# A one-core hybrid SSD and attention block: how q and k leave PSUM, where the first bias columns lie, and when eight modulation columns are computed

## The chip, the cores and the metric

The kernel runs on one core of a Trainium2 chip. A core has a matrix engine (TensorE, PE in the profile; its weight loads are shown as PEld), a vector engine (VectorE, DVE), an activation engine (ScalarE, ACT), a general engine (GpSimd, POOL) and a sync engine (SyncE, SP), which issues most of the DMAs here. Each engine takes its instructions strictly in the order in which the program lists them, and they wait for each other by semaphores. The metric is the device time of one execution in microseconds (us), taken as the median of several runs.

## The reference, cut to what matters

One layer with a state-space (SSD) group, an attention group and a feed-forward part. The change touches the attention group and the modulation vector `mod`, which is a product of a row vector with a matrix of 1024 x 6144.

```python
c_act = jax.nn.silu(c)
mod = (c_act @ w_ada[l] + b_ada[l])[:, None, :]
sh_m, sc_m, g_m, sh_f, sc_f, g_f = jnp.split(mod, 6, axis=-1)
h = rmsnorm(x, norm_mix_w[l]) * (1 + sc_m) + sh_m
z, xbc, dt_raw, q, k, v = jnp.split(h @ w_in[l], IN_SPLITS, axis=-1)
...
# chunk_attention: 8 heads of 64, chunks of 64 rows, own chunk + 8 before
scores = einsum('bcqhd,bckhd->bhcqk', qc, kb) * (ATTN_HEAD_DIM ** -0.5)
bias = rel_bias[:, rel_idx]          # clipped relative position
p = softmax(where(valid, scores + bias, min))
o = einsum('bhcqk,bckhd->bcqhd', p, vb)
```

The sequence has 1024 rows, the model 1024 columns, and everything is float32.

## The kernel before, in words

A product of two float32 matrices is made of three products of rounded parts (`mm3`, L79 to L82): each operand is split into a high part, rounded by an ACT copy, and a low part, which DVE computes as the operand minus the high part (`split`, L84 to L90).

The stages run in this order. **Stage 0** (about 0 to 97 us): x is loaded, normalized and transposed; the first 16 modulation columns are computed, one row of `w_ada` at a time, by `mod_col` (L136), which loads 512 KB by an SP DMA and reduces it on DVE against a row buffer `rowa`; and the q, k and v of head pairs 0 and 1 are computed from `w_first` in two halves of 512 rows (the `for hh in range(2)` loop), with four PSUM accumulators `accs`, n = 0 to 3, for q and k of pair 0 and of pair 1. **Attention** (about 97 to 280 us): `attention(p)` for the four head pairs; in each, four steps u of two blocks of 128 query rows (i = 2u and 2u + 1). `attn_scores` computes the scores of a block on PE (`scores`, L258), adds the bias and takes the row minimum of the negated sum on DVE (L494), takes the exponential on ACT (L497), the reciprocal on DVE (L499) and normalizes on POOL (L500). `attn_pv` transposes the result on PE (L526, L529), splits it (L89, L90) and multiplies it with v (L537, L538). While pair 1 and pair 2 run, `gemm_part` computes q, k and v of the next pair (`acc`, one PSUM bank; the second half of 512 rows can start only when the first has been taken out of it). **Convolution** (`conv_silu`, about 267 to 370 us) follows with 24 to 25 modulation columns between, and then the SSD part, the output projection and the feed-forward part, which the change doesn't touch.

Around the change:

- `evac_qkv` (L220) takes q, k or v of one pair and one half out of PSUM. The score product wants, for each of the two heads, a q tile whose one half of the partitions holds the high part and the other half the low part, and tiles `kh` and `kl` that hold the same 64 rows on both halves of the partitions. The accumulator has head 0 on partitions 0 to 63 and head 1 on 64 to 127. For q the kernel before uses two ACT instructions (L226) and two DVE instructions (L228) on 64 partitions each, and no DMA. For k it uses two ACT (L232), two DVE (L235), and four SP DMAs (L233, L236) that copy 64 x 512 numbers to the other half of the partitions. This is done 16 times: for q and k, four pairs, two halves.
- `attention` loads two bias tiles of 128 x 640 for its pair (L555), masks two corners on POOL (L556, L557), and the DVE of L494 reads them. The pools of attention are opened when those of stage 0 are closed, on the same memory.
- `rowb` is the second half of the tile `rows_`. It is used at the start (`diag`, until about 8 us) and again after the convolution (L846).
- In pair 3, `attention` calls `mod_col` `MODS` = (0, 1, 1, 5) times in its steps, into four free q/k buffers; each is placed behind the last reciprocal of the step's scores. After each convolution column tile, `conv_mods` calls it `CMODS` times.
- The order of the instructions on each engine is set when the program is built: a planner walks through the program with estimated durations and, on each engine, issues what is ready by its estimate, earlier program text first. GEMMs of a next stage are thus pulled forward to fill PE. [...]

Of the kernel before, what the change touches and what calls it, by code (L numbers as in the profile page):

```python
# [25 lines left out]
WZB = 4  # L26
PB = (2, 2, 0, 4)
GRID = 1.5 * 2.0 ** 17
MODS = (0, 1, 1, 5)
CMODS = (2, 3, 3, 3, 3, 3, 4, 4)  # L30
PRST = 4
GP, GPL = {0: (0,1), 2: (2,)}, ()
XL = (3, 4, 5, 6)
# [11 lines left out]
def f32(ap):  # L45
    return ap.bitcast(F32)
# [22 lines left out]
def tile_block(ctx: ExitStack, tc: tile.TileContext, x, ccol, pk, w_ada, w_first, w_ft, w_z,  # L69
               w_out, w_up, w_down, bias, fnw, out, dbg=None):  # L70
    nc = tc.nc
    V, A, T = (InOrder(tc, e) for e in (nc.vector, nc.scalar, nc.tensor))
    G = nc.gpsimd
# [28 lines left out]
    rowa, rowb = rows_[:, 0, :], rows_[:, 1, :]  # L102
# [33 lines left out]
    def mod_col(ft, t, at=None):  # L136
        nc.sync.dma_start(t, w_ada[ft])
        with tc.issue_after(at) if at else ExitStack():
            V.tensor_tensor_reduce(out=t, in0=t, in1=rowa, scale=1.0, scalar=0.0,
                                   op0=ALU.mult, op1=ALU.add, accum_out=modc[:, ft:ft + 1])  # L140
# [35 lines left out]
    es_at = ExitStack()  # L176
# [5 lines left out]
    s0 = es_0.enter_context(tc.tile_pool(name="s0", bufs=1, side="right"))  # L182
# [33 lines left out]
    def new_pair(p):  # L216
        qk[p] = {n: [qk_tile(F32R) for _ in range(2)] for n in ("q", "kh", "kl")}
        qk[p]["v"] = vv[:, :, p % 2]

    def evac_qkv(p, which, hh, ps, tmp, tps):  # L220
        d = qk[p]
        c = slice(hh * 512, hh * 512 + 512)
        rows = ((slice(0, 64), slice(64, 128)), (slice(64, 128), slice(0, 64)))
        if which == 0:
            for q, (r, o) in zip(d["q"], rows):
                A.activation(q[r, c], ps[r, :], AF.Copy, scale=0.125)  # L226
            for q, (r, o) in zip(d["q"], rows):
                V.scalar_tensor_tensor(q[o, c], ps[r, :], 0.125, f32(q[r, c]), op0=ALU.mult,  # L228
                                       op1=ALU.subtract)
        elif which == 1:  # L230
            for kh, (r, o) in zip(d["kh"], rows):
                A.activation(kh[r, c], ps[r, :], AF.Copy)  # L232
                nc.sync.dma_start(f32(kh[o, c]), f32(kh[r, c]))  # L233
            for kh, kl, (r, o) in zip(d["kh"], d["kl"], rows):
                V.tensor_tensor(kl[r, c], ps[r, :], f32(kh[r, c]), ALU.subtract)  # L235
                nc.sync.dma_start(f32(kl[o, c]), f32(kl[r, c]))  # L236
# [101 lines left out]
    for j in range(2):  # L338
# [9 lines left out]
                           op0=ALU.add, op1=ALU.mult)  # L348
# [34 lines left out]
    for hh in range(2):  # L383
        accs = [(ps0, ps0b)[n // 2].tile([P, 512], F32, tag="acc0", bufs=2, name="acc0") for n in range(4)]
        vps = [psv.tile([P, 2, 256], F32, tag=t, bufs=1, name="vps") for t in ("acc", "pv")]
        split_at = KT - (2, 4)[hh]
        tail = range(split_at, KT)
        for kt in range(KT):
            if hh == 0:
# [77 lines left out]
    pp = es_at.enter_context(tc.tile_pool(name="pp", bufs=8, side="right", reuse_waits="tile"))  # L467
    bp = es_at.enter_context(tc.tile_pool(name="bp", bufs=3, side="right", reuse_waits="tile"))
    ptp = es_at.enter_context(tc.tile_pool(name="ptp", bufs=1, side="right", reuse_waits="tile"))
    pst = es_p1.enter_context(tc.tile_pool(name="pst", bufs=1, space=PSUM, side="right",  # L470
                                           reuse_waits="tile"))
    ya = yp.tile([P, NT, 512], F32, tag="y", name="ya")
# [6 lines left out]
    def tp_tile():  # L479
        return pst.tile([P, 512], F32, tag="tp", bufs=2, name="tp")  # L480

    def attn_scores(p, i, bt):
        st, n, off, parts = s00 if p + i == 0 else scores(p, i)
        res = []
        for h in range(2):
            pt_ = p_tile()
            nm, rs = stat(), stat()
            if len(parts) == 1:
                src, bsl, dst = st[h][:, 0:n], bt[h][:, off:off + n], pt_[:, 0:n]
            else:  # L490
                src = st[h].rearrange("p (a b) -> p a b", a=2)[:, :, 0:320]
                bsl = bt[h].rearrange("p (a b) -> p a b", a=2)
                dst = pt_.rearrange("p (a b) -> p a b", a=2)
            V.tensor_tensor_reduce(out=dst, in0=src, in1=bsl, scale=-1.0, scalar=3e38,  # L494
                                   op0=ALU.add, op1=ALU.min, accum_out=nm)
# [4 lines left out]
            G.tensor_scalar(pv_, pv_, rr, 1.0, op0=ALU.mult, op1=ALU.mult)  # L500
            res.append(pt_)
        return res
# [47 lines left out]
    def attention(p, extra=()):  # L550
        extra = dict(extra)
        bt = []
        for h in range(2):
            t = bp.tile([P, 640], F32, tag="bias", name="bias")
            nc.sync.dma_start(t, bias[2 * p + h])  # L555
            G.memset(t[0:64, 576:640], -1e30)  # L556
            G.memset(t[64:128, 0:64], -1e30)  # L557
            bt.append(t)
        for u in range(4):
            pa = attn_scores(p, 2 * u, bt)  # L560
            pb = attn_scores(p, 2 * u + 1, bt)
            for fn in extra.get(u, ()):
                fn()
            if p == 3:
                if u < 2:
                    early[4 + 2 * u] = wu_pair(w_ft[4 + 2 * u], A, G)
                for _ in range(MODS[u]):
                    mod_col(todo.pop(0), mtq[len(todo) % 4], last_v[0])
            for h in range(2):
                attn_pv(p, u, h, pa[h], pb[h])  # L570

# [6 lines left out]
    def gemm_part(p, which):  # L578
        if which == 0:
            new_pair(p)  # L580
        if p == 2 and which < 2:
            with tc.issue_after(wpin[0].ins), tc.issue_after(wpin[1].ins):
                wh, wl = wu_pair(w_ft[8 + 3 * (p - 2) + which], A, V)
        else:
            wh, wl = wu_pair(w_ft[8 + 3 * (p - 2) + which], A, G)
        outs = [psv.tile([P, 512], F32, tag="acc", bufs=1, name="acc") for _ in range(2)]
        gemm_ft(wh, wl, outs)
        for hh in range(2):
            tmp = tps = None
# [16 lines left out]
        return last.ins  # L606

    part = lambda p, w: (lambda: gemm_part(p, w))
    attention(0)
    for p in (1, 2):  # L610
        attention(p, {u: [part(p + 1, w) for w in ws] for u, ws in GP.items()})
# [1040 lines left out]
```

## Time and profile before

| what | value |
|---|---|
| median of 3 runs | 1209.1 us (1207.89 to 1209.68) |
| the profiled execution | 1210.09 us, its span 1208.3 us |
| mean granted TensorE clock in it | 0.987 |
| PE busy | 1169.2 us, 97% of the span |
| DVE / ACT / POOL busy | 76% / 49% / 13% |
| DMA q/k copies (`qk<-qk`) | 32 of 128 KB, 2.2 us to landing |

The time outside the span (1.8 us) is start and end of the execution. In the tables of the profile, a group of instructions is named by its line, engine and operation, by what it writes and reads (`out<-in`), its shapes and its count; then come the busy time, the mean duration of one, and the idle time of the engine before it with what ended that idle time (`<-DVE qk L228` means: released by a DVE instruction of line 228 that wrote tile `qk`). A busy PE is not PE at its peak, since the ends of matmuls are modelled. PEclk is the granted clock of PE as a share of full speed.

### The profile page before, as it was taken

To read this page: it belongs to the slowest core of one execution; us is meant where nothing else is said; L and a number is where in the kernel's file an instruction comes from. 1 tells how busy PE (TensorE), PEld (TensorE's weight loads), DVE (VectorE), ACT (ScalarE), POOL (GpSimd) and SP (SyncE) were. 2 spreads that over 40 slices of the span, in tenths; PEclk is the share of its full clock that TensorE was granted. 3 is DMA by queue.
4 is the path that set the end of the run, shared out by engine and by line. 5 is a ranking of instruction groups with operands and counts; after the bars stand their busy time and mean duration, and the time that the engine had idled before them with its cause. 6 is when DMAs were issued, how large, how long until landed. Compare 5 with 4: busy or idle time off the path is not lost.

```text
span 1208.3 us, 15693 instructions
## 1 busy us (share of the span) xinstructions
PE 1169.2 (97%) x5823; PEld 980.0 (81%) x5823; DVE 921.6 (76%) x1380; ACT 597.4 (49%) x984; POOL 154.7 (13%) x175
## 2 busy tenths in 40 slices
PE   8999999989999889999999999999999999999996
PEld 6878887878879878888788888888888888888885
DVE  7847455686595878647999988898889779766986
ACT  6636454673243757477544443345343445433454
POOL 1103232440000345300000000000000000000522
PEclk8999999999999989999999999999999999999998
DMA  9613121311477312140232323322233278733443
GB/s 343 236 57 86 36 70 40 112 56 54 160 259 244 124 52 100 59 157 36 79 114 104 114 96 105 131 79 90 96 129 114 100 257 291 265 114 123 157 132 147
DMA packets 57804, 154.59 MB, mean 128 GB/s; under 512 B 5936, under 2 KB 6144, under 8 KB 56320
## 3 DMA queue, kind: packets, MB, share of 16 engines
q1 hardware_dynamic: 50672, 129.21, 31.6%
q10 hardware_dynamic: 7056, 24.38, 5.1%
q8 instruction: 46, 0.75, 0.2%
q14 instruction: 30, 0.25, 0.1%
HBM read 120.76 MB, written 28.61 MB: 124 GB/s over the span
## 4 chain that ended last, share of the span: by engine, by line
PE 68%; DVE 5%; DMA 2%; ACT 1%; issue 1%; POOL 0%; POOLq 0%; SPq 0%; DVEq 0%; ACTq 0%
PE wops L791 6%; PE dn L82 5%; PE dn L80 5%; PE dn L81 5%; PE uY L80 5%; PE uY L82 5%; PE uY L81 5%; PE uX L82 3%; PE uX L80 3%; PE uZ L81 3%; PE uZ L80 3%; PE uX L81 3%; PE uZ L82 3%; PE s L81 2%; PE s L80 2%; PE s L82 2%
## 5 line engine op out<-in xcount | busy, mean ns | idle before, releaser
L81 PE MATMUL dn<-w 128*128 128x512 f32 x296 | 108.1, 392 | 0.0
L80 PE MATMUL dn<-w 128*128 128x512 f32 x296 | 108.1, 392 | 0.0
L82 PE MATMUL dn<-w 128*128 128x512 f32 x296 | 100.3, 391 | 0.2 <-DVE w L90 0.2
L80 PE MATMUL uY<-tH,w 128*128 128x512 f32 x248 | 97.2, 392 | 0.0
L81 PE MATMUL uY<-tL,w 128*128 128x512 f32 x248 | 97.0, 391 | 0.0
L82 PE MATMUL uY<-tH,w 128*128 128x512 f32 x248 | 97.0, 391 | 0.0
L1513 POOL TENSOR_TENSOR ya<-ya,xs 128x512 f32<-128x512 f32 x4 | 17.2, 4336 | 557.6 <-ACT xs L1509 557.6
L89 ACT ACTIVATE w<-ya 128x1024 fp32r<-128x1024 f32 (+1 forms) x41 | 39.2, 957 | 87.4 <-PE uY L82 84.2
L791 PE MATMUL wops<-hH,yhl 128*128 128x512 f32 x224 | 72.7, 398 | 0.0
L82 PEld LDWEIGHTS dn<-w 128*128 128x128 f32 x296 | 55.4, 188 | 13.2 <-DVE w L90 1.1
L80 PEld LDWEIGHTS dn<-w 128*128 128x128 f32 x296 | 55.5, 188 | 12.4
L81 PEld LDWEIGHTS dn<-w 128*128 128x128 f32 x296 | 55.6, 188 | 12.2
L494 DVE CUSTOM_DVE_ANT_0 p<-s,bias 128x640 f32<-128x640 f32 (+4 forms) x64 | 40.6, 651 | 25.0 <-PE tp L526 11.7
L89 ACT ACTIVATE w<-xs 128x1024 fp32r<-128x1024 f32 (+1 forms) x41 | 39.1, 954 | 37.4 <-PE uY L82 33.3
L500 POOL TENSOR_SCALAR p<-p,st 128x640 f32<-128x640 f32 (+4 forms) x64 | 45.9, 722 | 76.4 <-DVE st L499 72.3
L82 PEld LDWEIGHTS uY<-tH,w 128*128 128x128 f32 x248 | 46.6, 188 | 10.4
L80 PEld LDWEIGHTS uY<-tH,w 128*128 128x128 f32 x248 | 46.6, 188 | 10.3
L81 PEld LDWEIGHTS uY<-tL,w 128*128 128x128 f32 x248 | 46.6, 188 | 10.2
L90 DVE TENSOR_TENSOR pt<-tp,pt 128x512 fp32r<-128x512 f32 (+2 forms) x72 | 42.1, 595 | 16.2 <-ACT pt L89 15.7
L80 PE MATMUL s<-hH,wh 128*128 128x512 f32 x128 | 50.2, 393 | 1.9 <-DVE ct L601 1.9
L1187 DVE SCALAR_TENSOR_TENSOR a<-cv,pkt,a 128x1023 f32<-128x1023 f32 (+1 forms) x40 | 51.1, 1279 | 0.1
L81 PE MATMUL s<-hL,wh 128*128 128x512 f32 x128 | 50.5, 394 | 0.0
(489 smaller groups left out, 3428.9 us busy)
## 6 DMA issues: line engine op xcount, KB each, us to landing
wos<-in_w_ada_dram SPq DMA_DIRECT2D x25, 512.0 KB, 4.8
gz<-a ACTq DMA_DIRECT2D x10, 1024.0 KB, 5.0
ya<-in_w_up_dram SPq DMA_DIRECT2D x11, 768.0 KB, 4.1
xs<-in_w_up_dram SPq DMA_DIRECT2D x11, 768.0 KB, 4.2
adat<-in_w_ada_dram SPq DMA_DIRECT2D x16, 512.0 KB, 6.1
raws<-in_w_ft_dram SPq DMA_DIRECT2D x14, 512.0 KB, 3.6
gy<-a ACTq DMA_DIRECT2D x10, 512.0 KB, 2.6
qk<-in_x_dram SPq DMA_DIRECT2D x8, 512.0 KB, 8.2
```

The lines of the kernel that those rows point to most:

```text
L80: T.matmul(ps, lh, rh, start=start, stop=False, skip_group_check=more)
L81: T.matmul(ps, lh, rl, start=False, stop=False, skip_group_check=more)
L82: T.matmul(ps, ll, rh, start=False, stop=stop, skip_group_check=more)
L89: i = A.activation(hi, src, AF.Copy) if ehi is A else ehi.tensor_copy(hi, src)
L90: return i, elo.tensor_tensor(lo, src, f32(hi), ALU.subtract)
L494: V.tensor_tensor_reduce(out=dst, in0=src, in1=bsl, scale=-1.0, scalar=3e38, op0=ALU.add, op1=ALU.min, accum_out=nm)
L500: G.tensor_scalar(pv_, pv_, rr, 1.0, op0=ALU.mult, op1=ALU.mult)
L791: i = op(*a, **k)
L1187: V.scalar_tensor_tensor(a[:, j:S], c[:, 0:S - j], w[2 - j], a[:, j:S], op0=ALU.mult, op1=ALU.add)
L1513: G.tensor_tensor(src, src, fnr[:, halves[1]], ALU.mult)
```

## The change

q and k leave PSUM with one ACT and one DVE instruction on all 128 partitions. For q, the low part goes to a staging tile and three DMAs then bring the quarters to their places; for k, six DMAs do it in the place of four. The staging tile is one half of a stage 0 tile (`junk`) for pairs 0 and 1, and a new tile `ev` (one buffer) for pairs 2 and 3. Two DMAs load columns 256 to 639 of the bias of pair 0 into `rowb`, and the first three blocks of pair 0 read them there; the full tiles are still loaded, for the blocks behind. The seven modulation columns of pair 3 are taken out, and eight are put into the steps of pairs 1 and 2, one in each step, with `rowb` as their single buffer; the last convolution tile has three and not four.

```diff
-MODS = (0, 1, 1, 5)
-CMODS = (2, 3, 3, 3, 3, 3, 4, 4)
+CMODS = (2, 3, 3, 3, 3, 3, 4, 3)
...
     def evac_qkv(p, which, hh, ps, tmp, tps):
         d = qk[p]
         c = slice(hh * 512, hh * 512 + 512)
-        rows = ((slice(0, 64), slice(64, 128)), (slice(64, 128), slice(0, 64)))
+        up, dn = slice(64, 128), slice(0, 64)
+
+        def move(dst, o, src, r, sc):
+            nc.sync.dma_start(f32(dst[o, c]), f32(src[r, sc]))
+
         if which == 0:
-            for q, (r, o) in zip(d["q"], rows):
-                A.activation(q[r, c], ps[r, :], AF.Copy, scale=0.125)
-            for q, (r, o) in zip(d["q"], rows):
-                V.scalar_tensor_tensor(q[o, c], ps[r, :], 0.125, f32(q[r, c]), op0=ALU.mult,
-                                       op1=ALU.subtract)
+            q0, q1 = d["q"]
+            lo = ev_tile()
+            A.activation(q0[:, c], ps, AF.Copy, scale=0.125)
+            V.scalar_tensor_tensor(lo, ps, 0.125, f32(q0[:, c]), op0=ALU.mult, op1=ALU.subtract)
+            move(q1, up, q0, up, c)
+            move(q1, dn, lo, up, slice(0, 512))
+            move(q0, up, lo, dn, slice(0, 512))
         elif which == 1:
-            for kh, (r, o) in zip(d["kh"], rows):
-                A.activation(kh[r, c], ps[r, :], AF.Copy)
-                nc.sync.dma_start(f32(kh[o, c]), f32(kh[r, c]))
-            for kh, kl, (r, o) in zip(d["kh"], d["kl"], rows):
-                V.tensor_tensor(kl[r, c], ps[r, :], f32(kh[r, c]), ALU.subtract)
-                nc.sync.dma_start(f32(kl[o, c]), f32(kl[r, c]))
+            (kh0, kh1), (kl0, kl1) = d["kh"], d["kl"]
+            A.activation(kh0[:, c], ps, AF.Copy)
+            for o in (up, dn):
+                move(kh1, o, kh0, up, c)
+            V.tensor_tensor(kl0[:, c], ps, f32(kh0[:, c]), ALU.subtract)
+            for o in (up, dn):
+                move(kl1, o, kl0, up, c)
+            for t in (kh0, kl0):
+                move(t, up, t, dn, c)
...
+        def ev_half():
+            if not evj:
+                t = s0.tile([P, D], F32R, tag="junk", name="evl")
+                evj.extend((t[:, 512:1024], t[:, 0:512]))
+            return evj.pop()
...
+    evp = es_at.enter_context(tc.tile_pool(name="evp", bufs=1, side="right", reuse_waits="tile"))
+    evs.append(lambda: evp.tile([P, 512], F32R, tag="ev", name="ev"))
...
+    def bias_early():
+        for h in range(2):
+            t = rowb[:, 384 * h:384 * h + 384]
+            nc.sync.dma_start(t, bias[h][:, 256:640])
+            G.memset(t[0:64, 320:384], -1e30)
+            be.append(t)
...
-            if len(parts) == 1:
+            if p == 0 and i < 3:
+                src, bsl, dst = st[h][:, 0:n], be[h][:, off - 256:off - 256 + n], pt_[:, 0:n]
+            elif len(parts) == 1:
...
+            if p in (1, 2):
+                mod_col(todo.pop(0), rowb, last_v[0])
             if p == 3:
                 if u < 2:
                     early[4 + 2 * u] = wu_pair(w_ft[4 + 2 * u], A, G)
-                for _ in range(MODS[u]):
-                    mod_col(todo.pop(0), mtq[len(todo) % 4], last_v[0])
...
+    bias_early()
     attention(0)
```

More of the change, by code (lines that the diff above doesn't have):

```diff
@@ L218, in new_pair, with ev_tile @@
         qk[p]["v"] = vv[:, :, p % 2]
+    evs = []
+    def ev_tile():
+        return evs[-1]()
     def evac_qkv(p, which, hh, ps, tmp, tps):
@@ L386, in tile_block @@
         split_at = KT - (2, 4)[hh]
+        evj = []
+        def ev_half():
[3 more added lines that the diff above has]
+            return evj.pop()
+        evs.append(ev_half)
         tail = range(split_at, KT)
@@ L480, in tp_tile @@
         return pst.tile([P, 512], F32, tag="tp", bufs=2, name="tp")
+    be = []
+    def bias_early():
[4 more added lines that the diff above has]
+            be.append(t)
     def attn_scores(p, i, bt):
```

## The prediction, made blind

> **What bounds the kernel now.** I read the page first (busy time, the chain that ended last), then PE's waits, then the busy time by stretch, and last the timelines of DVE, PE and SP in attention.
>
> ```profile
> PE 1169.2 (97%) x5823; PEld 980.0 (81%) x5823; DVE 921.6 (76%) x1380; ACT 597.4 (49%) x984; POOL 154.7 (13%) x175
> PE 68%; DVE 5%; DMA 2%; ACT 1%; issue 1%; POOL 0%; POOLq 0%; SPq 0%; DVEq 0%; ACTq 0%
> ```
>
> PE is busy for 97% of the span and carries the chain. The change removes no matmul, so it can gain only where PE stands still or where its clock is low, and it touches only the time to about 370 us.
>
> ```profile
> 50.00:97.00 47.00, 44.96 (x260) 37.92 (x259) 25.03 (x40) 20.22 (x32) 0.55 (x1) 1.00 0.25 66
> 97.00:127.00 30.00, 28.12 (x153) 23.21 (x151) 18.45 (x63) 18.52 (x47) 12.01 (x26) 0.94 0.19 61
> 127.00:182.00 55.00, 52.08 (x309) 45.29 (x307) 30.19 (x81) 31.91 (x73) 17.87 (x21) 1.00 0.20 61
> 182.00:240.00 58.00, 54.21 (x314) 46.44 (x314) 32.31 (x86) 32.68 (x73) 17.91 (x21) 0.99 0.21 66
> 240.00:280.00 40.00, 36.80 (x224) 31.38 (x223) 33.40 (x90) 24.05 (x60) 15.03 (x21) 0.98 0.23 73
> 280.00:370.00 90.00, 88.13 (x446) 74.44 (x446) 66.53 (x90) 33.55 (x50) 0.29 (x1) 1.00 0.52 175
> ```
>
> The columns are the stretch, its length, the busy time of PE, PEld, DVE, ACT and POOL, the granted clock, and the DMA share. The rows are about the end of stage 0, pairs 0, 1, 2 and 3, and the convolution. From 97 to 280 us PE idles for 30 - 28.12 + 55 - 52.08 + 58 - 54.21 + 40 - 36.80 = 11.8 us. That is the pool from which nearly all of a gain must come. DVE is 84% busy in pair 3 (33.40 of 40) and 55% in pairs 1 and 2 (30.19 of 55, 32.31 of 58).
>
> ```profile
> PE acc L80 <- DVE qk L228: 3.4, 4, 1.1
> PE acc L80 <- DVE qk L235: 2.2, 4, 1.1
> PE s L258 <- DVE st L494: 0.9, 3, 0.4
> PE tp L526 <- POOL p L500: 1.1, 1, 1.1
> PE pv L537 <- DVE ya L543: 0.8, 1, 0.8
> ```
>
> The first two rows are PE's waits up to 420 us, the third those from 97 to 127 us, the last two those from 240 to 280 us (total, times, longest). The largest item is the second half of a q or k GEMM, or the next part, that waits until DVE has taken the half before out of the one `acc` bank: 3.4 + 2.2 = 5.6 us in eight waits, 0.7 us each.
>
> **The change part by part.**
>
> **A. Taking q and k out of PSUM.**
>
> ```profile
> 114.82 1.20 ACT L226 ACTIVATE qk<-acc 64x512 fp32r<-64x512 f32 x2
> 116.97 1.39 DVE L228 SCALAR_TENSOR_TENSOR qk<-acc,qk 64x512 fp32r<-64x512 f32 x2
> 118.42 0.50 PE L80 MATMUL acc<-hH,wh 128*128 128x512 f32 x1 [0.98 <-DVE qk L228]
> 94.61 0.60 ACT L89 ACTIVATE v<-vps 128x512 fp32r<-128x512 f32 x1 [1.33 <-PE vps L62]
> 95.24 0.69 DVE L90 TENSOR_TENSOR v<-vps,v 128x512 fp32r<-128x512 f32 x1 [0.57 <-ACT v L89]
> ```
>
> Before, it is 1.20 us of ACT and 1.39 us of DVE, and PE starts 0.06 us after DVE's end (116.97 + 1.39 = 118.36). A split on 128 partitions out of PSUM costs 0.60 and 0.69 us, as much as one half does now. So each of the 16 times saves 0.60 + 0.70 = 1.3 us of the way from the last matmul to the free bank, and over the kernel 9.6 us of ACT and 11.2 us of DVE. In the eight waits of attention, 1.3 us is more than the longest wait (1.1). With the matmul order kept, all 5.6 us go. But the planner fills these waits with other matmuls by its own estimates, and with a shorter estimate it will put fewer of them there; what remains is the part by which its estimate is short, and that was made by four instructions and is now made by two. Ends: 0 and -5.6 us. I take -3.5 us, nearer the full end, because what is left of a wait after -1.3 us would have to be made anew. Late next is the matmul that the planner puts there.
>
> In stage 0, the other eight times, nothing of PE's waits lies on L228 or L235 (the first two rows hold only `acc L80` of attention); the cover is the tail matmuls of the other accumulators and v. I take 0 there.
>
> **The moves.** Instead of 32 there are 8 x (3 + 6) = 72 SP copies.
>
> ```profile
> qk<-qk SPq DMA_DIRECT2D x32, 128.0 KB, 2.2
> 79.46 8.19 SPq L233 DMA_DIRECT2D qk<-qk  x3
> 87.88 1.19 SPq L236 DMA_DIRECT2D qk<-qk  x2
> 94.69 0.55 SPq L233 DMA_DIRECT2D qk<-qk  x1
> 95.29 1.24 SPq L236 DMA_DIRECT2D qk<-qk  x2
> 97.33 19.97 SPq L555 DMA_DIRECT2D bias<-in_bias_dram  x5
> 100.51 0.29 DVE L494 CUSTOM_DVE_ANT_0 p<-s,bias 128x128 f32<-128x128 f32 x1 [1.86 <-POOL bias L556]
> 105.61 0.67 DVE L494 CUSTOM_DVE_ANT_0 p<-s,bias 128x512 f32<-128x512 f32 x1
> 152.61 1.40 DVE L235 TENSOR_TENSOR qk<-acc,qk 64x512 fp32r<-64x512 f32 x2
> 184.56 0.28 DVE L494 CUSTOM_DVE_ANT_0 p<-s,bias 128x128 f32<-128x128 f32 x1
> ```
>
> A copy takes about 0.6 us of SP (1.19 for two) and lands after 2.2 us. The last move of a q, and the last two of a k, must wait for earlier ones that read the rows which they overwrite, so q is complete two landings after DVE (4.4 us and some issue), where it needed none. This is hidden in attention: pair 2's last k is taken out at 152.61 us and its first block reaches DVE at 184.56 us; 4.4 us fit. SP waits some 1.7 us at such a move, with weight loads, bias loads and the new modulation loads behind it; weight loads are issued a whole GEMM part ahead. Cost 0; with the cover gone it is 2 to 4 us at the start of a pair. The one tight place is the end of stage 0, a rival below.
>
> **C. The first bias columns.** The first DVE instruction of attention starts at 100.51 us and waited for the POOL mask of the bias, whose load SP could issue only at 97.33 us, when the memory of stage 0 came free. The same memory gives the `p` tiles, so with the bias already in `rowb` it can start at 97.4 at the earliest, 3.1 us sooner. PE is fed with GEMM at that time, so the gain shows later: DVE and ACT, which set the pace from 103 to 118 us, are ahead, and the 0.9 us of PE waiting for L494 there go. Ends: +0.9 (as much again, if block 3 then waits for its full tile) and -1.9 us (all of PE's idle time from 97 to 127 us, 30 - 28.12, the 0.98 of A's wait among it); I take -0.7 us. The two loads and two masks (64 x 64 on POOL) cost nothing, as POOL is busy for 0.55 us in all of 50 to 97 us.
>
> **D. Pair 3 without its seven columns.**
>
> ```profile
> L139 DVE CUSTOM_DVE_ANT_0 qk<-qk,rows x7: 1194/1223/1732, 256.9 to 275.0; 128x1024 f32<-128x1024 f32 x7
> 256.90 1.21 DVE L139 CUSTOM_DVE_ANT_0 qk<-qk,rows 128x1024 f32<-128x1024 f32 x1
> 258.62 0.39 PE L537 MATMUL pv<-pt,v 128*128 128x256 f32 x1 [0.81 <-DVE ya L543]
> 263.70 1.19 DVE L139 CUSTOM_DVE_ANT_0 qk<-qk,rows 128x1024 f32<-128x1024 f32 x1
> 265.65 0.30 PE L526 MATMUL tp<-ident,p 128*128 128x128 f32 x1 [1.05 <-POOL p L500]
> 250.00:260.00 10.00, 8.72 (x58) 7.37 (x58) 8.88 (x26) 8.03 (x21) 3.70 (x5) 1.00 0.09 18
> 260.00:270.00 10.00, 8.78 (x54) 7.34 (x53) 9.41 (x28) 7.41 (x18) 6.08 (x7) 1.00 0.28 89
> ```
>
> Seven columns of 1.22 us go. Five run at the end under convolution GEMM, where PE doesn't wait: 0. The one at 256.90 stands right before PE's 0.81 us. The one at 263.70 stands beside 1.05 us that POOL ended, which it does not cause directly; but DVE is 89 and 94% busy there, and 1.2 us less pulls all that follows forward. PE idles 1.28 + 1.22 = 2.5 us in these 20 us. Ends 0 and -2.5; I take -1.6 us (0.81 and about the same from the second). In the convolution one column less saves 1.2 us of DVE, with no PE idle beside it that it would end: 0.
>
> **E. Eight columns in pairs 1 and 2.** They add 8 x 1.22 = 9.8 us of DVE, one behind the last reciprocal of each step. Behind it on DVE wait the splits of the transposed `p` (L90), for which PE waits.
>
> ```profile
> 148.70 0.42 DVE L543 TENSOR_TENSOR ya<-pv,tl 64x256 f32<-64x256 f32 x1 [4.63 <-ACT tl L542]
> 200.97 0.42 DVE L543 TENSOR_TENSOR ya<-pv,tl 64x256 f32<-64x256 f32 x1 [4.51 <-ACT tl L542]
> qk<-in_w_ada_dram SPq DMA_DIRECT2D x7, 512.0 KB, 4.8
> ```
>
> DVE has holes of about 4.5 us under the GEMMs, enough for a column each, and the load of 4.8 us fits between two steps (about 14 us apart: 55 or 58 us for four). If the planner uses the holes, the cost is 0; if each stands fully in PE's way, +9.8. The nearest row is pair 3: 0.81 to 1.86 us of PE idle beside seven columns, 0.12 to 0.27 us each; eight of them at 0.19 give +1.5 us, which I take.
>
> **B. The clock.**
>
> ```profile
> 118.42:122.50 4.08, 4.08 (x11) 3.24 (x12) 1.84 (x6) 1.68 (x5) 2.95 (x7) 0.58 0.24 78
> 237.00:242.50 5.50, 4.45 (x26) 4.23 (x25) 3.57 (x12) 3.41 (x10) 2.77 (x6) 0.69 0.99 380
> ```
>
> Twice the granted clock falls: 0.58 over 4.08 us and 0.69 over 5.50 us, which costs 4.08 x 0.42 = 1.7 and 5.5 x 0.31 = 1.7 us. Both follow stretches where PE waits often for short times, and A, C and D thin these out. In the second the DMA share is 0.99, part of it the columns' loads that the change takes away. Ends: -3.4 (both go) and +1.7 us (a third one comes in pairs 1 and 2); I take -1.0 us.
>
> The Trainium skill, in "TensorE: Matmul & The Clock Gate", section "Why this matters for your kernels", says otherwise: only an idle gap of more than about 3 us between matmuls sends the clock back. Here the trace disagrees, as no wait of PE quoted above is over 1.1 us and the clock fell all the same. By that rule the term B would be 0 and the sum 1.0 us smaller.
>
> **Sum:** -3.5 (A) - 1.0 (B) - 0.7 (C) - 1.6 (D) + 1.5 (E) = -5.3 us. The profiled execution took 1210.1 us (span 1208.3 and 1.8 around it) and would take 1204.8; it lies 1.0 us over the median of 1209.1, so I expect a median of 1203.8 us.
>
> **The rivals.** A measurement of this kernel can tell some 0.2%, or 2.4 us: faster is under 1206.7, slower over 1211.5.
>
> - *The columns stop PE* (slower). In pairs 1 and 2 each column stands in front of a split that PE waits for, at 1.22 us each, and the new waits bring a third clock dip. Then E is +9.8 and B +1.7: -3.5 + 1.7 - 0.7 - 1.6 + 9.8 = +5.7, or 1214.8 us. It is slower once a column costs PE 0.81 us (6.5 / 8). For it: DVE is in order, and steps u = 1 and 3 have no new GEMM part to cover. Against: DVE is 55% busy there, and in pair 3, at 84%, a column cost at most 0.27.
> - *The planner takes A back.* The waits for `acc` stay as long as they are, as fewer matmuls are put before them: -5.3 + 3.5 = -1.8, or 1207.3 us, no difference. For it: the waits are alike in size (0.5 to 1.1) in all eight places, as a systematic error of an estimate would be. Against: half of that error goes with half of the instructions.
> - *SP is late with the full bias.* From some 84 us on (an estimate: the q of this half comes out one step ahead of the k copies issued at 87.88) SP has 24 moves in place of 12; at 0.6 us they take 14.4 us, to 98.4, and with five waits for landings of 1.7 us to 106.9. The full tile is there 3.2 us later (100.51 - 97.33), at 110.1, and block 3 needs it at 105.61 or earlier: DVE waits up to 4.5 us. PE has GEMM for some; with 3.6 us lost and C gone: -5.3 + 0.7 + 3.6 = -1.0, or 1208.1 us. Against: the waits overlap with DVE's own pace, since a move cannot be issued before its ACT or DVE instruction is done anyhow.
> - *All waits go*: A -5.6, B -3.4, C -0.9, D -2.5, E 0, or -12.4: 1196.7 us. It would need an order that fits at every place.
> - *The clock does not follow the waits*: both dips stay, B is 0, the rest as forecast: -4.3, or 1204.8 us. For it: the second dip lies in the change from pair 2 to pair 3, where there are few GEMM matmuls left whatever DVE does. The rule of the Trainium skill named under B would give this time.
>
> **How the numbers follow.** The forecast (-5.3, with its own range of 1201 to 1206.5) has 0.40, the clock rival 0.14, all waits gone 0.12: faster 0.66. The planner rival 0.13 and the late bias 0.06: same 0.19. The columns 0.15: slower 0.15. The predicted time is that of the forecast, 1203.8 us. The range reaches from 1197 (the ideal sum) to 1213 (most of the way to the columns rival), and leaves out about 0.15.
>
> **What would show it.** A: the two rows of PE waiting for `acc` behind L228 and L235's successors fall from 5.6 us to some 2, and ACT and DVE instructions of these lines are 16 each and not 32. C: the first L494 starts near 97.5 us after the same number of matmuls. D: DVE under 8 us of 10 in the last blocks of pair 3, and the attention stretch (97 to 280) shorter by some 5 us. E: rows in which PE waits for L90 or L543 right behind a modulation column; more than 6 us of them would make me wrong. B: PEclk in the rows around 120 and 240 us. I should be wrong too if the order of the matmuls in attention is so different that none of these waits can be found again.

## The result, and the profile after

The kernel after takes 1206.37 us in the median of 17 runs, the kernel before, run beside it, 1208.0 (17 runs). The ratio is 0.9982, with a 95% interval of 0.9975 to 0.9989: 2.2 us faster (1.3 to 3.0), a little under the 0.2% that the prediction took as its limit between faster and the same, and less than half of the 5.3 us forecast. The profiled execution has a span of 1204.2 us (before 1208.3). Single executions of one kernel differ by some 2.5 us to either side of the median, so the 4.1 us between these two spans are not the size of the change; sizes below are taken from ratios, and places from the traces.

First, PE's waits from 97 to 420 us in the kernel after (total, times, longest):

```profile
PE tp L564 <- POOL p L535: 3.5, 2, 2.5
PE pv L572 <- DVE ya L578: 2.5, 1, 2.5
PE pv L573 <- DVE pt L89: 1.2, 2, 0.9
PE acc L79 <- DVE ev L236: 0.2, 1, 0.2
PE acc L79 <- DVE qk L245: 0.2, 1, 0.2
```

The waits for `acc`, 5.6 us in eight places before, are down to 0.4 in two. In their place stand two new ones: 3.5 us for POOL's normalization, and 2.5 us behind a sum into `ya`. The busy time by stretch, same columns as before:

```profile
50.00:97.00 47.00, 44.56 (x253) 37.39 (x254) 19.71 (x34) 17.43 (x27) 1.10 (x2) 1.00 0.37 94
97.00:127.00 30.00, 25.92 (x142) 22.43 (x141) 18.19 (x61) 16.94 (x44) 10.12 (x22) 0.89 0.51 135
110.00:120.00 10.00, 9.42 (x49) 8.77 (x49) 7.74 (x25) 7.03 (x18) 5.44 (x10) 0.69 0.06 22
127.00:182.00 55.00, 54.63 (x326) 47.94 (x325) 30.74 (x84) 29.67 (x68) 21.59 (x24) 1.00 0.38 102
182.00:240.00 58.00, 53.94 (x320) 46.80 (x320) 36.30 (x94) 31.35 (x73) 23.48 (x24) 0.99 0.39 116
240.00:280.00 40.00, 38.63 (x232) 33.02 (x232) 25.48 (x76) 25.59 (x61) 11.08 (x18) 0.97 0.00 1
```

Pair 1 is nearly full (PE 54.63 of 55, before 52.08) and pair 3 has gained (38.63 of 40, before 36.80; DVE 25.48 in place of 33.40). Pair 2 has not (53.94 of 58, before 54.21), and the first 30 us of attention have lost: PE 25.92 us in place of 28.12, with a mean granted clock of 0.69 from 110 to 120 us. The next rows, a timeline of SP, PE and POOL at that place and then three stretches of busy time, show why:

```profile
95.67 7.64 SPq L230 DMA_DIRECT2D qk<-qk  x11
103.35 0.58 SPq L590 DMA_DIRECT2D bias<-in_bias_dram  x1
104.69 0.95 PE L271 MATMUL s<-qk 128*128 128x384 f32 x4
107.13 0.14 POOL L591 MEMSET bias<- 64x64 f32 x1 [6.02 <-DMA bias<-in_bias_dram]
107.57 0.48 POOL L535 TENSOR_SCALAR p<-p,st 128x256 f32<-128x256 f32 x1
108.10 0.44 PE L564 MATMUL tp<-ident,p 128*128 128x128 f32 x2 [2.46 <-POOL p L535]
109.60 0.14 POOL L591 MEMSET bias<- 64x64 f32 x1 [1.55 <-DMA bias<-in_bias_dram]
110.04 0.48 POOL L535 TENSOR_SCALAR p<-p,st 128x256 f32<-128x256 f32 x1
110.57 0.69 PE L564 MATMUL tp<-ident,p 128*128 128x128 f32 x2 [1.09 <-POOL p L535]
105.00:109.00 4.00, 1.54 (x9) 1.13 (x8) 1.42 (x7) 1.58 (x6) 0.77 (x3) 1.00 0.82 257
109.50:116.00 6.50, 5.43 (x22) 5.24 (x23) 4.43 (x15) 3.88 (x11) 3.32 (x9) 0.50 0.14 59
116.50:120.00 3.50, 3.49 (x26) 3.05 (x24) 3.31 (x13) 3.00 (x8) 2.20 (x3) 1.00 0.02 5
```

SP is busy with moves of q and k until 103.35 us and only then issues the full bias of pair 0 (before: 97.33). POOL's program has the mask of that tile ahead of the normalizations of block 1, whose bias is the early one and long there. POOL stands still for 6.02 us until the tile has landed, with the normalizations behind it, although DVE had their reciprocals done at 105.15 and 105.97 us; then once more for 1.55 us for the second head's tile (DVE reads both tiles in block 3 before a third mask runs at 110.45 us, so the two are pair 0's). PE waits for both, 2.46 and 1.09 us. Behind the first of these waits, at 109.3 us, the clock falls to 0.50 and stays there until 116.2; the 0.69 is the mean of that over ten microseconds.

Stage 0 is longer too. The first matmul into `acc` starts at 98.61 us (97.13 before). The queue of SP near the start, before and then after:

```profile
7.21 0.33 SPq L397 DMA_DIRECT2D raws<-in_w_first_dram  x1
9.87 1.47 SPq L137 DMA_DIRECT2D adat<-in_w_ada_dram  x2
```

```profile
7.37 0.33 SPq L419 DMA_DIRECT2D raws<-in_w_first_dram  x1
8.74 1.59 SPq L511 DMA_DIRECT2D rows<-in_bias_dram  x2
10.97 1.61 SPq L136 DMA_DIRECT2D adat<-in_w_ada_dram  x2
```

The planner put the two loads of the early bias at 8.74 us, as soon as `rowb` is free, although their data is wanted at 98.81 us. From 10 to 40 us the DMA share is 0.99 to 1.03, so these 393 KB stand in front of loads that stage 0 waits for.

Last, two of the eight columns in pairs 1 and 2:

```profile
182.22 1.21 DVE L138 CUSTOM_DVE_ANT_0 rows<-rows 128x1024 f32<-128x1024 f32 x1
183.35 0.68 DVE L89 TENSOR_TENSOR pt<-tp,pt 128x512 fp32r<-128x512 f32 x1
184.09 0.39 PE L573 MATMUL pv<-pt,v 128*128 128x256 f32 x1 [0.93 <-DVE pt L89]
236.24 1.66 DVE L138 CUSTOM_DVE_ANT_0 rows<-rows 128x1024 f32<-128x1024 f32 x1
237.93 0.42 DVE L578 TENSOR_TENSOR ya<-pv,tl 64x256 f32<-64x256 f32 x1
238.50 0.35 PE L572 MATMUL pv<-pt,v 128*128 128x256 f32 x1 [2.49 <-DVE ya L578]
238.00:243.00 5.00, 4.23 (x22) 4.06 (x22) 2.94 (x12) 1.75 (x6) 1.30 (x3) 0.66 0.01 2
```

Both are those of the last step of a pair. Behind the first a split of `p` waits on DVE, behind the second the sum into `ya` that frees the one `pv` bank, and PE waits for these: 0.93 and 2.49 us. The granted clock is 0.66 in the 5 us from 238 us on, but that is no sign of the column: the kernel before, which has no column there, has 0.66 in the same 5 us.

So three theories stood after the result. **1**: taking q and k out in two instructions is worth more than forecast, and part of it is lost where the 24 moves at the end of stage 0 make the full bias late and POOL, in order, holds back work that is ready. **2**: the early bias loads, costed at nothing, cost 1.5 to 2 us of stage 0 because they are hoisted into the part where the DMAs are full. **3**: the eight columns cost more than pair 3 gains. Against each stood a rival that the part is harmless and the time lies elsewhere.

### The profile page after: what moved, and what is told of

The parts are those of the page before. It is cut to its first block, busy times and chain, and to the rows that moved or that the text cites. A ratio compares the mean times of both kernels' runs of the same rounds, so it can differ in the third digit from the quotient of the medians.

```text
span 1204.2 us, 15722 instructions
## 1 busy us (share of the span) xinstructions
PE 1168.7 (97%) x5823; PEld 980.8 (81%) x5823; DVE 909.1 (75%) x1364; ACT 587.5 (49%) x968; POOL 156.5 (13%) x177
## 4 chain that ended last, share of the span: by engine, by line
PE 85%; DVE 8%; issue 3%; DMA 2%; ACT 1%; SPq 1%; POOL 0%; POOLq 0%; DVEq 0%; ACTq 0%
PE wops L827 6%; PE dn L81 5%; PE dn L79 5%; PE dn L80 5%; PE uY L79 5%; PE uY L81 5%; PE uY L80 5%; PE uX L81 3%; PE uX L79 3%; PE uZ L80 3%; PE uZ L79 3%; PE uX L80 3%; PE uZ L81 3%; PE s L79 3%; PE s L80 3%
## 5 line engine op out<-in xcount | busy, mean ns | idle before, releaser
L535 POOL TENSOR_SCALAR p<-p,st 128x640 f32<-128x640 f32 (+4 forms) x64 | 49.3, 776 | 108.3 <-DVE st L534 95.2
L88 ACT ACTIVATE pt<-tp 128x512 fp32r<-128x512 f32 (+2 forms) x72 | 36.8, 525 | 29.9 <-PE tp L561 15.4
```

Source lines behind the costliest of these rows:

```text
L88: i = A.activation(hi, src, AF.Copy) if ehi is A else ehi.tensor_copy(hi, src)
```

## The experiments

Each ratio is to the kernel before, timed beside the kernel on the same chip, with its 95% interval; 0.001 is 1.2 us. Kernels that are compared with each other across groups of runs are compared by these ratios.

### The parts, each alone

**Taking out and moves alone.** The kernel before with the new `evac_qkv` and its `ev` tiles; bias and columns as before.

> Only the new way of taking q and k out of PSUM, with its moves; bias and modulation columns as before. Theory 1 (the new way ends PE's waits for the acc bank, 5.6 us, but its 24 moves at the end of stage 0 keep SP from the bias loads, 97.3 us in the kernel before and 103.4 in the changed one): acc waits under 1 us, bias loads issued near 103 us, first L494-like DVE instruction at 106 us or later, and about -1.5 us against before in the end (1206.5). Rival (the moves are hidden and the loss in the changed kernel comes from elsewhere): bias at 98 us and -5 us (1203).

Measured: 1207.38 us, ratio 0.9993 (0.9981 to 1.0005). The only wait for `acc` left is 0.2 us, stage 0 is not longer (first `acc` matmul at 97.3 us), and PE is busy 55.00 of 55 us from 127 to 182. All of it is lost again right at the start of attention (SP, then DVE):

```profile
101.29 0.58 SPq L589 DMA_DIRECT2D bias<-in_bias_dram  x1
105.32 0.29 DVE L528 CUSTOM_DVE_ANT_0 p<-s,bias 128x128 f32<-128x128 f32 x1 [6.50 <-POOL bias L590]
```

The bias is issued 4 us later than before and the first block starts 4.8 us later (100.51 before). From 97 to 127 us PE has 4.1 us of waits for that DVE line (0.9 before), and the clock is 0.82 from 100 to 110 us and 0.84 from 110 to 120.

**The early bias alone.** The kernel before with `bias_early` and its use in the first three blocks.

> Only the first bias columns in the idle row buffer; q and k by the old way, columns as before. Theory 1: with 12 moves SP is free by 97 us, the first DVE instruction of attention starts near 98 us in place of 100.5, the full tiles are there before they are needed, and the time falls by about 1 us (1207). Rival (an earlier start is only given back by the order of the matmuls): within 0.3 us of before.

Measured: 1210.21 us, ratio 1.0019 (1.0007 to 1.0031): slower. The loads stand at 8.50 us, and the first `acc` matmul comes at 99.01 us.

**The columns alone.** The kernel before with `mod_col` in pairs 1 and 2 in place of pair 3.

> Only the modulation columns moved to pairs 1 and 2. Theory 1: DVE in pair 3 is freed (-1.5 us there) but two or three of the eight columns stop PE for 1 to 2.5 us each in pairs 1 and 2, so +1 to +2 us against before (1209 to 1210). Rival (the columns fall into holes): -1.5 us (1206.5).

Measured: 1211.22 us, ratio 1.0028 (1.0015 to 1.0041): slower. Here it is the first column's load into `rowb` that is hoisted, to 8.31 us, and the first `acc` matmul comes at 98.86 us. The waits for `acc` stay (3.4 and 2.1 us); the splits behind the columns of the last steps of pairs 1 and 2 stop PE for 0.93 and 1.15 us, and the clock is 0.66 from 240 to 250 us.

**All, but the old way in stage 0.** The kernel after, where pairs 0 and 1, taken out at the end of stage 0, are done by the old instructions and copies.

```diff
-        if which == 0:
+        if which == 0 and p < 2:      # the two branches of the kernel before
+            ...
+        elif which == 0:
```

> The changed kernel, but pairs 0 and 1 are taken out of PSUM by the old way (12 copies at the end of stage 0 in place of 24); pairs 2 and 3 by the new one. Theory 1: the bias loads are issued near 97.5 us, POOL does not wait 6 us for the mask, PE's 3.5 us of waiting for POOL and the clock dip of 0.69 from 110 to 120 us go, and the time is 3 to 5 us under the changed kernel (1202). Rival (the stall at 105 to 111 us has another cause): as the changed kernel, 1206.

Measured: 1203.54 us, ratio 0.9960 (0.9945 to 0.9974), better than the kernel after. A window and POOL's first mask:

```profile
97.00:127.00 30.00, 28.98 (x174) 24.54 (x173) 18.85 (x65) 18.51 (x49) 12.12 (x26) 1.00 0.35 104
102.46 0.14 POOL L605 MEMSET bias<- 64x64 f32 x1 [0.81 <-DMA bias<-in_bias_dram]
```

With 12 copies in place of 24 moves the full bias is there in time, POOL idles 0.81 us and not 6.02, and PE is busy 28.98 of 30 us at full clock. The hoisted loads (8.39 us; first `acc` matmul 99.16) and the waits behind the last columns are still there.

### The early loads

The next three put the two early bias loads behind the last load of x on SP's queue, at some 37.5 us, and change nothing else:

```diff
-            nc.sync.dma_start(t, bias[h][:, 256:640])
+            with tc.issue_after(xl[-1].ins):
+                nc.sync.dma_start(t, bias[h][:, 256:640])
```

> The kernel before with the early bias columns alone (1.0019), their loads put behind the last load of x. Theory 2a: first acc matmul near 97.2 us in place of 99.01; the loss of 2.3 us is gone and the ratio is 0.9995 to 1.0005, less if the earlier start of the first DVE instruction brings what the prediction gave it (0.7 us: 0.9994). Theory 2b: ratio 1.002 as without the pin.

> The kernel after, with the two early bias loads put on the queue behind the last load of x (at some 39 us, in place of 8.7 us). Theory 2a (loads that the planner hoists into the first 40 us, where the DMA share is 1.0, delay the loads behind them and cost 1.5 to 2 us of stage 0): the first matmul into acc comes at 97.0 to 97.4 us in place of 98.61, and the ratio falls by 0.0012 from 0.9982 to 0.997 (about 1204.5). Theory 2b (the later first acc matmul has another cause, such as the larger number of moves or another order of PE): it stays at 98.6 and the ratio at 0.998.

> The kernel with the old way of taking q and k out for pairs 0 and 1 (0.9960), and its two early bias loads put behind the last load of x. Theory 2a: first acc matmul 97.0 to 97.6 us in place of 99.16, ratio 0.9943 to 0.995 (about 1202). Theory 2b: 99.2 us and 0.996.

Measured, without and with the pin:

| kernel | ratio without | ratio with pin | first `acc` matmul, us |
|---|---|---|---|
| before + early bias | 1.0019 | 0.9998 (0.9988 to 1.0008) | 99.01, then 97.54 |
| after | 0.9982 | 0.9960 (0.9948 to 0.9973) | 98.61, then 96.39 |
| old way in stage 0 | 0.9960 | 0.9936 (0.9923 to 0.9949) | 99.16, then 96.77 |

Theory 2 holds three times: 0.0021, 0.0022 and 0.0024, or 2.5 to 2.9 us, of which 1.5 to 2.4 are seen at the end of stage 0. It was put a little too low. A single trace is not exact to a microsecond at this place, but the two groups do not mix: the first `acc` matmul comes at 98.61 to 99.40 us in the five profiles that have a hoisted load, and at 96.39 to 97.84 in the nine that have none. The 393 KB at the 407 GB/s that the kernel after moves from 10 to 20 us are only 1.0 us; where the rest comes from was not tried. The first row says a second thing: with the loads out of the way the early bias alone is worth nothing that can be told (0.2 us, between a loss of 1.0 and a gain of 1.5), although DVE's first instruction of attention does start earlier (97.74 us, before 100.51).

### The end of stage 0

**Masks later on POOL.** The kernel after, with the masks of pair 0's two full tiles behind the normalizations of block 2.

```diff
+        if p == 0 and i == 2:
+            with tc.issue_after(g_.ins):
+                for t in bt:
+                    mask(t)
```

> The kernel after, with the masks of the two full bias tiles of pair 0 put on POOL behind the normalizations of block 2, and nothing else changed. Theory 1a (in the kernel after, POOL is in order and its mask, which waits for the late full bias, holds up normalizations that were ready, and PE waits for those and its clock falls): the waits of PE on POOL p between 105 and 112 us (2.46 + 1.09 us) go, the clock of 110 to 120 us rises from 0.69 to above 0.9, and with 3 to 4 us gained the ratio to before is 0.995 to 0.996 (about 1203). Theory 1b (the late full bias itself is the limit, since block 3 needs it): the wait turns up at block 3's first DVE instruction instead, PE waits there, and the ratio stays 0.998.

Measured: 1205.39 us, ratio 0.9974 (0.9963 to 0.9985), between the two expectations, and not told apart from the kernel after (0.9982). POOL and PE:

```profile
110.98 0.14 POOL L590 MEMSET bias<- 64x64 f32 x1 [3.65 <-DMA bias<-in_bias_dram]
112.06 0.69 PE L565 MATMUL tp<-ident,p 128*128 128x128 f32 x2 [3.06 <-POOL p L535]
```

Block 1 is free, but a mask of a third bias tile, that of pair 1's first head, which the planner also puts early, has taken the place: it now holds up block 2, for 3.06 us, and the clock from 110 to 120 us is 0.66. The masks of pair 0, behind block 2 as asked, then keep DVE waiting for 3.32 us at block 3. So this run moved the stall and did not remove it.

**The full bias on another queue.** The kernel after with pinned early loads, and pair 0's two full tiles loaded from ACT's queue, not behind the moves.

```diff
-            nc.sync.dma_start(t, bias[2 * p + h])
+            (nc.sync if p else nc.scalar).dma_start(t, bias[2 * p + h])
```

> The kernel after with its early bias loads pinned (0.9960), and the two full bias tiles of pair 0 loaded from the queue of ACT, so that they do not stand behind the 24 moves of q and k on SP. Theory 1c (what the new way of taking q and k out costs at the end of stage 0 is only that the full bias and its mask come late): the first mask comes before 101 us, the waits of PE on POOL p (3.6 us in two) go, and the ratio falls to that of the old way in stage 0 with pinned loads, 0.9936, or below it. Theory 1d (the moves themselves cost, since q and k of pair 0 are complete later, or since the order of PE is another): the ratio stays near 0.996.

Measured: 1206.26 us, ratio 0.9981 (0.9971 to 0.9991): worse than without (0.9960), a miss for both expectations. The first masks came at 101.05 and 102.66 us, but (SP, POOL, PE):

```profile
104.75 0.58 SPq L593 DMA_DIRECT2D bias<-in_bias_dram  x1
108.33 0.14 POOL L594 MEMSET bias<- 64x64 f32 x1 [5.33 <-DMA bias<-in_bias_dram]
108.75 1.49 POOL L538 TENSOR_SCALAR p<-p,st 128x256 f32<-128x256 f32 x3
109.29 0.69 PE L567 MATMUL tp<-ident,p 128*128 128x128 f32 x2 [5.64 <-POOL p L538]
```

The bias load that is left on SP at that time can only be pair 1's. Its mask now stands in front of block 1's normalizations, POOL idles 5.33 us for it, and PE waits 5.64 us.

**And that mask later.** The same kernel, with one thing more: pair 1's masks stand behind the first normalization of pair 0's block 4.

```diff
+            with tc.issue_after(gn[0]) if p else ExitStack():
                 G.memset(t[0:64, 576:640], -1e30)
                 G.memset(t[64:128, 0:64], -1e30)
```

> The kernel of the run with the full bias of pair 0 on the queue of ACT (0.9981), and one thing more: the masks of pair 1's bias tiles stand on POOL behind the first normalization of block 4 of pair 0. In that run the mask for which POOL stood still (5.33 us idle, until 108.33 us) was that of pair 1's first tile, whose load SP issued only at 104.75 us, behind the moves; block 1's normalization stood behind it, and PE waited 5.64 us. Theory 1e (in-order POOL, with a mask of a late bias tile ahead of normalizations that are ready, is all that the new way of taking q and k out costs at the end of stage 0): the wait of PE on POOL p at 103 to 109 us falls from 5.6 to below 1 us, PE is busy over 9 of 10 us from 100 to 110 us, and 4 to 5.6 us come back: a ratio of 0.9933 to 0.9948, as with the old way in stage 0 (0.9936). Theory 1f (something else holds block 1 to 3 back as well, the moves or the order of PE): PE waits there for another engine and the ratio stays above 0.996.

Measured: 1200.32 us, ratio 0.9934 (0.9921 to 0.9947), 5.7 us faster than without that line. PE's waits from 97 to 127 us, and the busy time there:

```profile
PE s L271 <- DVE st L534: 0.7, 2, 0.4
PE tp L571 <- POOL p L540: 0.2, 1, 0.2
```

```profile
100.00:110.00 10.00, 9.39 (x52) 7.46 (x50) 6.26 (x26) 5.87 (x18) 4.11 (x11) 1.00 0.78 220
110.00:120.00 10.00, 9.45 (x61) 8.28 (x61) 9.60 (x29) 9.65 (x24) 5.75 (x10) 1.00 0.26 74
```

The wait for POOL is 0.2 us, the clock 1.00, and the time is that of the old way in stage 0 (0.9936). Theory 1 holds in its narrow form: the 24 moves themselves cost nothing there that can be told (the two ratios differ by 0.0002, each known to 0.0013). What cost was a late load whose mask stood in POOL's order ahead of ready work. Late masks alone, with the bias still on SP's queue, were not run.

### The columns

Both start from the kernel with the old way in stage 0 and pinned loads (0.9936).

**Columns back where they were** (seven in pair 3, the eighth in the convolution):

> The kernel with the old way for pairs 0 and 1 and pinned bias loads (0.9936), with the modulation columns where the kernel before has them (seven in pair 3, one more in the convolution). Theory 3a (the eight columns in pairs 1 and 2 cost more than pair 3 gains): the columns alone gave +3.4 us, some 1.7 of them by the hoisted load; so taking them back gives 1.7 us, a ratio of 0.992 to 0.9925. Theory 3b (with the other parts there, pair 3 gains more than the columns cost, as the prediction had it, 1.6 against 1.5 or better): the ratio is 0.9936 to 0.9955.

Measured: 1201.5 us, ratio 0.9944 (0.9932 to 0.9957). So moving the columns is worth 1.0 us, less than the two intervals can tell from nothing (2.2 us); theory 3 (a loss of 1.7 us) doesn't hold. With the hoisted load, which this run doesn't have, taken at the 2.5 to 2.9 us that the bias loads cost, the 3.4 us that the columns lost alone also come down to about 0.7 us.

**No column in the last step of pairs 1 and 2** (the two are done in the convolution):

```diff
-            if p in (1, 2):
+            if p in (1, 2) and u < 3:
```

> The kernel with the old way for pairs 0 and 1 and pinned bias loads (0.9936), with no column in the last step of pairs 1 and 2; the two are done in the convolution. Theory 4a (it is the column in the last step, where no GEMM is left for PE, that stops PE): the wait of 2.0 us behind the column near 230 us goes, the clock of 230 to 250 us rises from 0.91 to above 0.97, and the ratio falls to 0.9910 to 0.9920. Theory 4b (the waits there come from the change of pairs, with or without the column): the waits stay and the ratio is 0.9930 to 0.9940.

Measured: 1202.82 us, ratio 0.9949 (0.9936 to 0.9962): not faster. PE's longest wait in attention (97 to 280 us) is 2.0 us with eight columns, and in this kernel:

```profile
PE pv L589 <- ACT pt L88: 1.2, 1, 1.2
```

The wait behind the column goes, and the first matmul of the convolution comes 1.5 us sooner (255.22, after 256.71), although this trace's attention begins 1.0 us later. But at the first matmul behind the output projection it is 1.0 us late (553.38, after 552.41). So theory 4a was right on the wait, and the gain was given back later: PE has a wait of 2.3 us for `zs` behind the convolution that the kernel with eight columns doesn't have, and the clock falls once more there than in that kernel (0.50 for 3.4 us from 390.5 us on). On the clock theory 4a isn't shown: it does rise from 0.91 to 1.00 from 230 to 250 us, but the kernel after with pinned loads has 1.00 there with the column and its wait of 2.0 us, and the kernel with the columns where they were has 0.92 without.

### One step at a time

With 1208.5 us for the kernel before:

| kernel | ratio | step, us |
|---|---|---|
| before + early bias, pinned | 0.9998 | -0.2 |
| + new way for pairs 2 and 3 (columns as before) | 0.9944 | -6.5 |
| + columns moved | 0.9936 | -1.0 |
| + new way for pairs 0 and 1, bias on ACT's queue, late masks of pair 1 | 0.9934 | -0.2 |
| bias and masks as in the kernel after | 0.9960 | +3.1 |
| early loads not pinned: the kernel after | 0.9982 | +2.7 |

By the intervals, the first step has an uncertainty of 1.2 us and each of the others of some 2 us. The kernel after thus gains 8 us and gives 5.8 back, in two places apart from those where it gains.

## Why the prediction was right or wrong

**The time** was forecast as 1203.8 us and is 1206.4; faster, but by 2.2 us and not by 5.3. Of the runs, the one that has all parts of the change and neither of the two losses stands at 1200.3. That the time still lies close to the forecast is luck: A gave 3.0 us more than its term, and two things that the sum held at nothing took 5.8 back.

**A (taking q and k out: -3.5)** was right in its mechanism and too small. The 0.60 and 0.69 us of ACT and DVE per half were as forecast (0.60 and 0.68), and with pairs 2 and 3 alone the time falls by 6.5 us, against 5.6 us of waits; the difference is within the uncertainty. The prediction held back because the planner might put fewer matmuls into the waits. It didn't: 0.2 to 0.4 us of the waits are left in every kernel with the new instructions. The rival "the planner takes A back" is refuted.

**The moves (0)** is one of the two steps that failed. In attention they are hidden, as forecast. At the end of stage 0 they are not, and the place was named: the rival "SP is late with the full bias", with 0.06. Its times were close (a tile at 110.1 us forecast; the masks of pair 0's tiles end at 107.5 and 109.95), and so was its price (3.6 us; measured 3.1). What it had wrong is the way: it let DVE wait at block 3, which needs the tile, and argued that DVE's own pace would cover some. In the trace POOL waits at block 1, which doesn't need the tile. The prediction judged POOL by its busy time, and missed that an instruction that waits blocks its engine, whatever its share.

**C (early bias: -0.7)** measures -0.2 once its loads are pinned, within its bounds. DVE's first instruction starts at 98.81 us, 1.7 us sooner in the kernel after, though its stage 0 ends later. **"The two loads and two masks cost nothing"** is the other step that failed: it looked at POOL from 50 to 97 us and not at the queue and the part of stage 0 in which the planner would place the loads. They cost 2.7 us. The profile of before shows the DMAs full there (a share of 0.98 to 1.03 from 10 to 40 us); the step needed only the question of when `rowb` becomes free.

**D (-1.6) and E (+1.5)** summed to -0.1 and, with the column in the convolution, measure -1.0 with an uncertainty that takes in both. Apart they were not measured. Pair 3 shows D (PE 38.63 of 40, before 36.80). One reading under D was wrong in the kernel before: the column at 263.70 us does cause the wait of 1.05 us that POOL ended.

```profile
262.67 0.80 POOL L500 TENSOR_SCALAR p<-p,st 128x640 f32<-128x640 f32 x1 [0.92 <-DVE st L499]
263.94 1.62 POOL L500 TENSOR_SCALAR p<-p,st 128x640 f32<-128x640 f32 x1 [0.47 <-DVE st L499]
```

POOL's normalization, begun while the column ran, took 1.62 us in place of 0.80, and PE waited for it. That wait, 1.0 to 1.1 us, is in all five profiles with columns in pair 3 and in none of the nine without.

E is in the trace at the two columns of the last steps, 0.93 and 2.49 us of waits, 3.4 in all where 1.5 was forecast for all eight (3.4 is an upper bound, as the kernel before has waits of up to 0.79 us at the end of pair 2 too); no other single wait of PE from 127 to 280 us is longer than 0.7 us. The rival "the columns stop PE" holds in these two places, and far from its price of 9.8.

**B (clock: -1.0)** rested on two dips of the one profiled execution of the kernel before, and the record speaks against their belonging to the kernel. Of its 79 executions timed beside the experiments, 34 have a mean granted clock of 0.987, as the profiled one had, with a median of 1209.55 us, and 32 have 0.990 or 0.991, with medians of 1207.55 and 1206.12. And the kernel before with the pinned early bias, whose waits for `acc` and whose columns are those of before, was profiled at 1.00 from 97 to 280 us, with neither dip. So a saving to be had from the clock could not be read from that trace alone; the rival that the clock doesn't follow the waits had more for it than 0.14. In the profile of after, the second dip has stayed, and in place of the first there is one of twice the length, at 109.3 us. The runs show what that one goes with: where PE waits for POOL early in attention the clock fell in all four profiles that have such a stall, and not at that place where the stall was gone. By the rule of the Trainium skill in "TensorE: Matmul & The Clock Gate", section "Why this matters for your kernels", a drop takes an idle gap of more than about 3 us. That is again not what the trace shows: the longest wait ahead of the fall at 109.3 us is 2.46 us, and that ahead of the one at 239.0 is 2.49. Where the wait for POOL is over 3 us, as in the runs with the masks behind block 2 (3.06) and with the bias on ACT's queue (5.64), the clock falls too.

## What to carry to other kernels

A transfer that is wanted late and may be issued early need not be free (here it cost 2.5 to 2.9 us): look up when its destination becomes free, where a planner will put its issue, and how full the DMAs are at that time, and pin it behind the loads that are wanted first. An engine with a busy share of 13% can still hold the critical path by order alone: for every instruction that waits for a transfer, list what is ready behind it on its engine, and when a transfer is delayed, follow it to such instructions, also those of a later stage that the planner has pulled forward. Where parts of a change act at different places, measure each alone and then with its cover restored; here the two parts that lost alone cost nothing that could be told, and the gain was larger than the whole change showed.

## What the runs showed of the hardware

The mean clock of a kernel differs between its executions on one chip (0.987 or 0.990 to 0.991 for the kernel before), and some 2 to 3 us with it. Inside an execution, a granted clock such as 0.69 or 0.91 is a mean: read in windows of half a microsecond, the clock in all 14 profiles, from 95 to 440 us, is 1.00 or 0.50 but for the windows in which it changes, and it is 0.50 for 3.4 us or for two or three times that. So a fall costs 1.7 us or a multiple, and not an amount in proportion to the idle time before it. Beside one wait of 5.64 us (full bias on ACT's queue) it was one such stretch, from 109.0 to 112.4 us; behind the wait of 2.46 us in the kernel after it was two, from 109.3 to 116.2; behind waits of 2.90 and 0.70 us at the same place with pinned loads, one. No run here tells what makes the difference.

The same column reduction on DVE took 1.20 to 1.31 us in most places, but 1.43 to 1.73 in others, such as 236.24 us in the kernel after. No run was made for this, but in every profile the long ones begin while POOL is at work:

```profile
193.62 2.41 POOL L89 TENSOR_TENSOR wl<-raws,wh 128x1024 fp32r<-128x1024 f32 x1 [6.53 <-ACT wh L88]
195.38 1.73 DVE L138 CUSTOM_DVE_ANT_0 rows<-rows 128x1024 f32<-128x1024 f32 x1
```

Here POOL's instruction has 0.65 us left when the column begins, and the column takes 0.53 us longer than 1.20. At 236.24 us 0.59 are left, and the column takes 0.46 longer. Where the column begins first, it is POOL's instruction that takes longer, as in the two rows shown under D. That one engine waits there for the other fits all these rows; it is read from their times and was not tried.
